# Scaling attention probabilities on another engine, and turning two heads of a short branch at once

## The chip, the cores and the metric

The kernel runs on one core of a Trainium2 chip. The core has TensorE (PE in the profile: matrix products and transposes, with weight loads listed apart as PEld), VectorE (DVE), ScalarE (ACT), GpSimd (POOL) and SyncE (SP, which here issues every DMA). The metric is the device time of one launch in microseconds (us), lower is better. A measurement of this kernel is told as the median of its runs.

## The reference, cut to what matters

One decoder block on 1024 tokens of width 1024, all in float32: a normalised and modulated input goes through one wide projection; part of its columns feed 16 attention heads in 2 groups of 8, part a state-space mixer (SSD); the two are merged and projected, and a gated feed-forward layer follows. The change concerns the attention. Each query attends in three branches, and each branch is weighted by its own learned gate:

```python
s_c = einsum('btgjd,bngd->bgjtn', qb, k_cmp) * scale          # compressed keys, 63 of them
p_c = masked_softmax(s_c, cmp_end[None, :] <= t[:, None])
o_c = einsum('bgjtn,bngd->btgjd', p_c, v_cmp)
...
p_s = masked_softmax(s_s, m_s)                                # selected blocks
o_s = einsum('bgjtk,bgtkd->btgjd', p_s, vg)
...
p_w = masked_softmax(s_w, m_w)                                # sliding window of 512
o_w = einsum('bgjtk,bkgd->btgjd', p_w, vwb)
o = gb[..., 0:1] * o_c + gb[..., 1:2] * o_s + gb[..., 2:3] * o_w
```

With 1024 tokens, 16 blocks of 64 keys and 16 blocks chosen, the selected branch sees every earlier key.

## The kernel before, in words

The program has a projection stage (to about 260 us), an attention stage (about 260 to 1340 us), the SSD stage (to about 1860 us) and the feed-forward tail. Attention works in 32 units: group `g`, tile `i` of 128 queries, and half `hq` of the group's heads, so 4 heads of 128 queries each. A unit has three branches: `br` 0 (selected, `i + 1` tiles of 128 keys), `br` 1 (window, at most 5 tiles) and `br` 2 (compressed, 64 columns of which 63 count).

For branches 0 and 1, `score` makes for each head the product of queries and keys (`S`, two matmuls, since values are kept as a high and a low part), adds the mask and finds the row's extreme on VectorE (L1707, tile `P`), and takes the exponential in place on ScalarE with its row sums (L1711). After the fourth head, one reciprocal of the sums (L1717) and four instructions `scale` (L1720), one a head, multiply the 128 x n probabilities in place by the inverse sum and by the gate, two numbers a row. `score_cmp` does the same for the 4 heads of branch 2 in one tile `Pc` of 128 x 4 x 64.

`value_step` then turns the probabilities: PE transposes one 128 x 128 block of each of 4 heads into a tile `tp` (L1787); ScalarE copies `tp` rounded into the first half of a pair (L1790), VectorE subtracts that to get the second half (L1791, both named `kv` since the pairs lie in the buffer of keys and values). For branch 2 the block is 64 columns wide, so `tp` has 64 rows in use, again 4 transposes. `products` multiplies each half by the values and sums all tiles of the unit in one PSUM tile `o` (L1018): two matmuls of 512 columns a step, with 64 rows of `cvc` (compressed values) for branch 2 and 128 rows of `kv` otherwise.

The order on all engines is fixed when the program is built, by a planner (`Flow`). It walks through a model of time: each operation has a cost in us written beside it, times a reserve of 1.15 on ScalarE and VectorE and 1.2 on GpSimd, and a latency behind it. PE takes what is ready of the streams `products`, `scores` and `values`, in that rank, and a background stream `F` fills the rest: the projections of the SSD inputs (`fps`) and what follows them, such as the convolution, three instructions of L1064 and one of L1080 on VectorE for each 128 x 512 block of 24 of them. Every engine then runs its own list strictly in order. In the attention stage GpSimd computes the low parts of weights (L311, `wlo`) and, in 8 stretches (`mod_rows`), row sums of `w_ada`: four products (L1276, `wada`) and eight sums (L1279, `acc`), whose input comes by DMA. The probabilities of branch 0 have 4 buffers (tags a1 and a2), those of branch 1 another 4 (tag b): a buffer is free again when the last transpose of its branch has run.

Of the kernel before, what the change touches and what calls it, by code (L numbers as in the profile page):

```python
# [37 lines left out]
K_MLE, K_TGT, K_COS, K_SIN, K_RV, K_ID, K_END = 0, 128, 256, 320, 384, 392, 520  # L38
# [186 lines left out]
class Kern:  # L225
# [93 lines left out]
    def rope(self, x, nh, t):  # L319
# [3 lines left out]
        cb = self.kc[:, K_COS + 8 * t:K_COS + 8 * t + 8][:, None, :].to_broadcast(sh)  # L323
        sb = self.kc[:, K_SIN + 8 * t:K_SIN + 8 * t + 8][:, None, :].to_broadcast(sh)
# [34 lines left out]
    def startup(self):  # L359
# [70 lines left out]
        self.kcop = D(1.5, [], self.load_constants)  # L430
# [110 lines left out]
    def projections(self):  # L541

        nc, a, wk, dr, cp = self.nc, self.a, self.wk, self.dr, self.cp
        self.kc = wk.tile([128, K_ID], F, name="kc")
# [4 lines left out]
        self.tgt = self.kc[:, K_TGT:K_TGT + 128]  # L549
# [28 lines left out]
                          ("kv", 0), ("kv", 1))] + [Stream(self.token_blocks())])  # L578

# [39 lines left out]
    def q_evac(self, b, t0, ps, op):  # L619
# [15 lines left out]
        r = V(1.65, [x, self.kcop], rot)  # L635
        d = D(0.7, [r], store)
# [3 lines left out]
    def kv_evac(self, kind, t0, ps, op):  # L640
# [34 lines left out]
        r = V(1.75, [k1, self.kcop], rot)  # L675
        self.turns.append((kind, t0, [(kk, r)] + ([(vs, v1)] if kind == 0 else [])))
# [87 lines left out]
    def gates_dt(self):  # L764
# [67 lines left out]
        for lt, dst in ((self.mle, self.eac), (self.tgt, self.etl), (self.ones, self.edc)):  # L832
            ps = self.buf("t", [128, 256], "cum")
            op = yield ([dop, ps], 0.43, lambda lt=lt, ps=ps: nc.tensor.matmul(ps.t, lt, daf(), start=True, stop=True))
# [35 lines left out]
    def compress(self):  # L870
# [3 lines left out]
        self.cvc = wk.tile([64, 2, 2, 64], FR, name="cvc")  # L874
# [5 lines left out]
    def compress_part(self, m):  # L880
# [62 lines left out]
        else:  # L943
            for g in range(2):
                vp = self.buf("t", [64, 64], "vcp")

                def mm(g=g, vp=vp):
                    for t in range(2):
                        nc.tensor.matmul(vp.t, hs[:, t, g], w2[:, t], start=t == 0, stop=t == 1)

                op = yield (ev + [c["d2"], vp], 0.22, mm)
                y = A(0.11, [op], lambda g=g, vp=vp: nc.scalar.activation(self.cvc[:, g, 0], vp.t, AF.Copy))
                self.cvcop = V(0.14, [y], lambda g=g, vp=vp: nc.vector.tensor_sub(self.cvc[:, g, 1], vp.t, self.cvc[:, g, 0]))
                vp.until(self.cvcop)
            w2.until(op)
# [51 lines left out]
    def products(self, units):  # L1007
# [3 lines left out]
        for u in units:  # L1011
            o = self.buf("o", [128, 4, 128], f"o{u.nm}")
            for n in range(u.total):
                while not self.pv:
                    yield None
                vst, rows, pair, hi, lo = self.pv.pop(0)
                for m, need in ((0, hi), (1, lo)):
                    op = yield ([need, o], 0.22, lambda n=n, m=m, vst=vst, rows=rows, pair=pair: nc.tensor.matmul(  # L1018
                        o.t, vst(), pair()[m][:rows], start=n + m == 0, stop=n == u.total - 1 and m == 1))
# [31 lines left out]
    def background(self):  # L1051
# [7 lines left out]
        def finish_x(ps, op, ft, h):  # L1059
# [566 lines left out]
class Unit:  # L1626
# [51 lines left out]
    def score(self, br, h):  # L1678
# [315 lines left out]
```

## Time and profile before

| | |
|---|---|
| median of 3 runs | 2702.74 us (2699.96 to 2707.79) |
| the profiled execution, its own time | 2705.52 us |
| its span from first to last instruction | 2703.7 us |
| mean granted TensorE clock | 0.977 of full speed |
| busy: PE / DVE / ACT / POOL | 95% / 64% / 43% / 25% of the span |

The page gives busy time and idle time by engine over the whole span; the stage that the change touches is 40% of it, so views of the stretch from 260 to 1340 us are used where a number is to be about that stage. A granted clock of 1.0 means 2.4 GHz, 0.5 means 1.2 GHz. The time of a matmul runs to its modelled end, so the distance between the starts of neighbouring matmuls tells what one costs in a row.

### The profile page before, as it was taken

What the parts mean: (1) busy time and instruction counts of PE and PEld (TensorE: products, weight loads), DVE (VectorE), ACT (ScalarE), POOL (GpSimd) and SP (SyncE); (2) the same over time, 40 slices, a digit from 0 to 9 for tenths busy, and PEclk for the clock granted to TensorE, in tenths of its full rate; (3) what the DMA queues carried; (4) which work ended last, traced back from release to release, by engine and by line L of the source; (5) the groups of instructions that cost most, each with busy time, mean ns of one, the idle gap of its engine ahead of it and who ended that gap; (6) DMA issues with size and microseconds to landing.
All of it is one profiled execution on the core that took longest, in us unless ns stands there. A gap on an engine that the chain in (4) does not pass through costs nothing.

```text
span 2703.7 us, 38173 instructions
## 1 busy us (share of the span) xinstructions
PE 2581.8 (95%) x14098; PEld 2185.0 (81%) x14098; DVE 1737.9 (64%) x4053; ACT 1152.5 (43%) x2458; POOL 664.0 (25%) x397
## 2 busy tenths in 40 slices
PE   6999999989998999999998999989999999999997
PEld 5999778878887888887877888769988888888885
DVE  7644987887886888877557579877722333333336
ACT  4322665556564655665545355542621111111113
POOL 2112222131222232312242322212122112222223
PEclk8999999999999999999998999989999999999999
DMA  6434232222223232212455544335221111111111
GB/s 234 142 105 143 85 86 63 64 78 71 63 67 126 86 92 73 90 43 71 138 164 190 188 139 129 106 122 171 73 77 40 39 47 47 47 47 47 47 55 63
DMA packets 206555, 253.95 MB, mean 94 GB/s; under 512 B 15256, under 2 KB 150040, under 8 KB 205856
## 3 DMA queue, kind: packets, MB, share of 16 engines
q1 hardware_dynamic: 206368, 251.51, 29.9%
q8 instruction: 111, 1.82, 0.3%
q14 instruction: 76, 0.62, 0.1%
HBM read 195.75 MB, written 55.71 MB: 93 GB/s over the span
## 4 chain that ended last, share of the span: by engine, by line
PE 79%; DVE 13%; DMA 3%; ACT 3%; issue 2%; SPq 0%; POOL 0%; DVEq 0%; ACTq 0%; POOLq 0%
PE fps L280 6%; PE gu L280 6%; PE fps L282 6%; PE fps L281 6%; PE gu L281 6%; PE gu L282 6%; PE o L1018 5%; PE tp L1787 4%; PE S L1702 4%; DVE P L1720 3%; PE dps L282 3%; PE dps L281 3%; PE dps L280 3%; PE yd L1905 2%; PE tokps L282 2%
## 5 line engine op out<-in xcount | busy, mean ns | idle before, releaser
L1569 DVE TENSOR_TENSOR x<-x,dps 128x512 f32<-128x512 f32 x176 | 120.9, 687 | 248.8 <-PE dps L282 248.6
L280 PE MATMUL gu<-m_hi,whi_w 128*128 128x512 f32 x704 | 279.8, 397 | 0.0
L281 PE MATMUL gu<-m_lo,whi_w 128*128 128x512 f32 x704 | 276.2, 392 | 0.0
L282 PE MATMUL gu<-m_hi,wlo_w 128*128 128x512 f32 x704 | 274.6, 390 | 0.0
L1790 ACT ACTIVATE kv<-tp 128x512 fp32r<-128x512 f32 (+1 forms) x296 | 172.9, 595 | 228.0 <-PE tp L1787 204.9
L311 POOL TENSOR_TENSOR wlo_w<-raw_w,whi_w 128x1024 fp32r<-128x1024 f32 x44 | 109.5, 2509 | 533.3 <-ACT whi_w L309 533.3
L1791 DVE TENSOR_TENSOR kv<-tp,kv 128x512 fp32r<-128x512 f32 (+1 forms) x296 | 196.7, 684 | 51.2 <-ACT kv L1790 50.0
L1018 PE MATMUL o<-kv 128*128 128x512 f32 x528 | 193.4, 420 | 12.5 <-DVE kv L1791 9.7
L1711 ACT ACTIVATE P<-P,sm 128x640 f32<-128x640 f32 (+7 forms) x256 | 186.5, 730 | 33.7 <-DVE sm L1707 32.4
L1702 PE MATMUL S<-kv,Q 128*128 128x384 f32 (+5 forms) x768 | 185.8, 344 | 6.7 <-DVE sm L1707 6.5
L1720 DVE TENSOR_SCALAR P<-P,sm,gate 128x640 f32<-128x640 f32 (+7 forms) x256 | 188.5, 800 | 1.2
L1787 PE MATMUL tp<-id,P 128*128 128x128 f32 x1056 | 157.9, 277 | 9.5 <-DVE Q L1666 5.9
L280 PE MATMUL fps<-hT_hi,whi_x 128*128 128x512 f32 x384 | 159.7, 416 | 4.0 <-ACT xs L1105 3.3
L282 PEld LDWEIGHTS gu<-m_hi,wlo_w 128*128 128x128 f32 x704 | 132.3, 188 | 33.0
L1787 PEld LDWEIGHTS tp<-id,P 128*128 128x128 f32 x1056 | 128.3, 142 | 37.5 <-issue 11.2
L280 PEld LDWEIGHTS gu<-m_hi,whi_w 128*128 128x128 f32 x704 | 132.1, 188 | 29.9
L281 PEld LDWEIGHTS gu<-m_lo,whi_w 128*128 128x128 f32 x704 | 131.8, 187 | 30.3
L282 PE MATMUL fps<-hT_hi,wlo_x 128*128 128x512 f32 x384 | 152.6, 397 | 0.0
L281 PE MATMUL fps<-hT_lo,whi_x 128*128 128x512 f32 x384 | 152.5, 397 | 0.0
L280 PE MATMUL fps<-whi_z,hT_hi 128*128 128x256 f32 x512 | 150.8, 295 | 0.9 <-ACT u L1067 0.6
L1702 PEld LDWEIGHTS S<-kv,Q 128*128 128x128 f32 x768 | 129.8, 194 | 24.0 <-DVE sm L1707 9.9
L1707 DVE CUSTOM_DVE_ANT_0 P<-S,kb 128x256 f32<-128x256 f32 (+5 forms) x256 | 120.5, 493 | 42.7 <-PE tp L1787 32.8
(342 smaller groups left out, 7046.7 us busy)
## 6 DMA issues: line engine op xcount, KB each, us to landing
wada<-w_ada SPq DMA_DIRECT2D x40, 512.0 KB, 4.3
ac<-acd SPq DMA_DIRECT2D x32, 512.0 KB, 4.9
raw_x<-w_in SPq DMA_DIRECT2D x24, 512.0 KB, 5.1
raw_w<-w_gate SPq DMA_DIRECT2D x22, 512.0 KB, 4.3
raw_w<-w_up SPq DMA_DIRECT2D x22, 512.0 KB, 3.8
rawd<-w_down SPq DMA_DIRECT2D x22, 512.0 KB, 3.8
xsd<-xs SPq DMA_DIRECT2D x32, 256.0 KB, 2.4
raw_z<-w_in SPq DMA_DIRECT2D x16, 512.0 KB, 4.7
```

Source lines behind the costliest of these rows:

```text
L280: mm(ps, lh, rh, start=k == 0, stop=False)
L281: mm(ps, lh, rl, start=False, stop=False)
L282: mm(ps, ll, rh, start=False, stop=k == kt - 1)
L1018: op = yield ([need, o], 0.22, lambda n=n, m=m, vst=vst, rows=rows, pair=pair: nc.tensor.matmul(o.t, vst(), pair()[m][:rows], start=n + m ...
L1569: e = V(0.6, [op], lambda ps=ps, t=t, cs=cs: nc.vector.tensor_tensor(self.x1[:, t, cs], self.x1[:, t, cs], ps.t, op=OP.add))
L1702: mm(sp[:, :w], q, kvb.kv[:, br, r, first + c0:first + c1], start=r == 0, stop=r == 1)
L1707: nc.vector.tensor_tensor_reduce(P[:, c0:c1], sp[:, :w], k.kb[:, m0:m0 + w], scale=-1.0, scalar=sm[:, 0, h:h + 1] if p else 3.0e38, op0=OP ...
L1711: ex = A(0.26 + 0.8333e-3 * n, [mx], lambda: nc.scalar.activation(P[:, :n], P[:, :n], AF.Exp, bias=sm[:, 1, h:h + 1], scale=-1.0, accum_ou ...
L1720: nc.vector.tensor_scalar(P[:, :n], P[:, :n], sm[:, 3, m:m + 1], k.gate[:, i, self.h0 + m, br + 1:br + 2], op0=OP.mult, op1=OP.mult)
L1787: nc.tensor.transpose(tp[:rows, h], P, k.id)
L1790: hi = A(0.48, [op, pair], lambda: nc.scalar.activation(pair()[0][:rows], tp[:rows], AF.Copy))
L1791: lo = V(0.6, [hi], lambda: nc.vector.tensor_sub(pair()[1][:rows], tp[:rows], pair()[0][:rows]))
```

## The change

Four edits. First, `scale` runs on GpSimd and is booked there at 0.25 + 1.08e-3 n us. Second, branch 2 turns two heads with one transpose: two neighbouring heads of `Pc` are one block of 128 columns, so a step has 2 transposes and a `tp` of 128 x 256, and the copies of the pair shrink to 256 columns. The values of that branch lie in `cvc` once in the upper 64 rows and once in the lower 64, with zeros in the other half, and each half of the pair is multiplied by both, 256 columns each, into every second head of `o`. Third, `compress_part` makes these doubled values (a doubled `hs2`, a memset on GpSimd). Fourth, to make room for them, the rotary tables and one mask move from the constants into a buffer of tag a1, which is free between the start and the attention; and the planner's costs for the convolution and for the products are raised.

```diff
             def scale(m=m, P=self.P[br, m][0]):
-                nc.vector.tensor_scalar(P[:, :n], P[:, :n], sm[:, 3, m:m + 1], k.gate[:, i, self.h0 + m, br + 1:br + 2],
+                nc.gpsimd.tensor_scalar(P[:, :n], P[:, :n], sm[:, 3, m:m + 1], k.gate[:, i, self.h0 + m, br + 1:br + 2],
                                         op0=OP.mult, op1=OP.mult)
-            self.P[br, m] = self.P[br, m][0], V(0.2 + 0.55e-3 * n, [e], scale)
+            self.P[br, m] = self.P[br, m][0], G(0.25 + 1.08e-3 * n, [e], scale)
...
+        n = 2 if br == 2 else 4
+        c = slice(0, 128 * n)
...
         def trans():
-            for h in range(4):
-                P = self.P[2, 0][0][:, h] if br == 2 else self.P[br, h][0][:, j * 128:(j + 1) * 128]
-                nc.tensor.transpose(tp[:rows, h], P, k.id)
+            for h in range(n):
+                P = self.P[2, 0][0][:, 2 * h:2 * h + 2].rearrange("p h n -> p (h n)") if br == 2 \
+                    else self.P[br, h][0][:, j * 128:(j + 1) * 128]
+                nc.tensor.transpose(tp[:, h * 128:h * 128 + 128], P, k.id)
...
+                def product(m, n=n, vst=vst, pair=pair, o=o, u=u):
+                    if vst is None:
+                        for r in range(2):
+                            nc.tensor.matmul(o[:, r::2], self.cvc[:, u.g, r].rearrange("n r d -> n (r d)"),
+                                             pair()[m][:, 0:256], start=False, stop=False)
...
-                    op = yield ([need, o], 0.22, lambda n=n, m=m, vst=vst, rows=rows, pair=pair: nc.tensor.matmul(
+                    op = yield ([need, o], 0.23 if vst else 0.24, lambda m=m, product=product: product(m))
...
-            c = V(2.25, [a0, a1, e], conv)
+            c = V(2.5, [a0, a1, e], conv)
...
-            f = V(0.66, [th], lambda: nc.vector.scalar_tensor_tensor(u.t, xr[:, 3:], 1.0, u.t, op0=OP.add, op1=OP.mult))
+            f = V(0.75, [th], lambda: nc.vector.scalar_tensor_tensor(u.t, xr[:, 3:], 1.0, u.t, op0=OP.add, op1=OP.mult))
...
-        nc.sync.dma_start(self.kc, a["kc"][:, 0:K_ID])
+        nc.sync.dma_start(self.kc, a["kc"][:, 0:K_COS])
+        nc.sync.dma_start(self.kt.t, a["kc"][:, K_COS:K_ID])
```

On VectorE near the end of the attention of the second group (unit `7_0`, branch 1; `Pc` and `st` belong to its branch 2, `S_7_1` to the next unit) the list before reads:

```order
L1717 RECIPROCAL sm_7_0_13026<-sm_7_0_13026 128x4
L1791 TENSOR_TENSOR kv_8653<-tp_7_0_13189,kv_8653 128x512
L1720 TENSOR_SCALAR P_7_0_13111<-P_7_0_13111,sm_7_0_13026,gate 128x640
L1720 TENSOR_SCALAR P_7_0_13116<-P_7_0_13116,sm_7_0_13026,gate 128x640
L1720 TENSOR_SCALAR P_7_0_13145<-P_7_0_13145,sm_7_0_13026,gate 128x640
L1720 TENSOR_SCALAR P_7_0_13172<-P_7_0_13172,sm_7_0_13026,gate 128x640
L1747 RECIPROCAL st_7_0_13162<-st_7_0_13162 128x4
L1748 TENSOR_TENSOR st_7_0_13162<-st_7_0_13162,gate 128x4
L1749 TENSOR_TENSOR Pc_7_0_13194<-Pc_7_0_13194,st_7_0_13162 128x256
L1791 TENSOR_TENSOR kv_8653<-tp_7_0_13234,kv_8653 128x512
```

In the changed program the same stretch of VectorE's list (L1754 is the reciprocal of the sums, L1784 to L1786 the scaling of `Pc`, L1828 the subtraction) reads:

```order
L1754 RECIPROCAL sm_7_0_12952<-sm_7_0_12952 128x4
L1784 RECIPROCAL st_7_0_13104<-st_7_0_13104 128x4
L1785 TENSOR_TENSOR st_7_0_13104<-st_7_0_13104,gate 128x4
L1786 TENSOR_TENSOR Pc_7_0_13121<-Pc_7_0_13121,st_7_0_13104 128x256
L1828 TENSOR_TENSOR kv_8506<-tp_7_0_13152,kv_8506 128x512
```

The four scalings stood ahead of the scaling of the compressed branch and of the next subtractions, and are gone from this list. On GpSimd, in the last of the 8 stretches of `mod_rows`, the list before has only the products and sums of `w_ada`:

```order
L1276 TENSOR_TENSOR wada_13309<-wada_13309,sc 128x1024
L1279 TENSOR_TENSOR acc_13221<-acc_13221,wada_13309 128x512
L1276 TENSOR_TENSOR wada_13345<-wada_13345,sc 128x1024
L1279 TENSOR_TENSOR acc_13221<-acc_13221,wada_13309 128x512
L1279 TENSOR_TENSOR acc_13221<-acc_13221,wada_13345 128x512 x2
```

At the same place of GpSimd's list in the changed program (unit `7_1`, branch 0; L1757 is `scale`, L1313 and L1316 are the products and sums) there stands:

```order
L1757 TENSOR_SCALAR P_7_1_13268<-P_7_1_13268,sm_7_1_13117,gate 128x1024
L1313 TENSOR_TENSOR wada_13331<-wada_13331,sc 128x1024
L1313 TENSOR_TENSOR wada_13366<-wada_13366,sc 128x1024
L1316 TENSOR_TENSOR acc_13278<-acc_13278,wada_13331 128x512
L1757 TENSOR_SCALAR P_7_1_13275<-P_7_1_13275,sm_7_1_13117,gate 128x1024
L1316 TENSOR_TENSOR acc_13278<-acc_13278,wada_13331 128x512
L1757 TENSOR_SCALAR P_7_1_13308<-P_7_1_13308,sm_7_1_13117,gate 128x1024
L1316 TENSOR_TENSOR acc_13278<-acc_13278,wada_13366 128x512
L1757 TENSOR_SCALAR P_7_1_13333<-P_7_1_13333,sm_7_1_13117,gate 128x1024
```

The scalings of one branch now lie between products that wait for a DMA.

## Rows read from the trace of the kernel before

**Rows 1.** The page: its first line, and busy time by engine over the span.
```profile
span 2703.7 us, 38173 instructions
PE 2581.8 (95%) x14098; PEld 2185.0 (81%) x14098; DVE 1737.9 (64%) x4053; ACT 1152.5 (43%) x2458; POOL 664.0 (25%) x397
```
**Rows 2.** Busy time of each engine by stretch of the attention stage: stretch and its length, then busy us (and instructions) of PE, PEld, DVE, ACT, POOL, the granted TensorE clock, DMA share, GB/s. The last row is a stretch of the fifth, asked for by itself.
```profile
260.00:400.00 140.00, 130.69 (x662) 105.01 (x661) 124.94 (x285) 90.41 (x234) 40.95 (x29) 0.96 0.31 88
400.00:600.00 200.00, 190.17 (x1165) 165.84 (x1163) 167.62 (x355) 113.50 (x260) 50.56 (x33) 0.96 0.23 67
600.00:800.00 200.00, 192.96 (x1208) 169.04 (x1209) 170.99 (x373) 120.39 (x247) 52.54 (x34) 0.98 0.24 70
800.00:1000.00 200.00, 189.02 (x1182) 164.18 (x1181) 154.73 (x369) 112.28 (x300) 45.46 (x29) 0.97 0.31 97
1000.00:1200.00 200.00, 194.81 (x1123) 166.44 (x1122) 168.77 (x390) 119.30 (x259) 56.07 (x36) 1.00 0.25 76
1200.00:1340.00 140.00, 136.95 (x707) 111.74 (x705) 98.12 (x218) 78.98 (x168) 36.67 (x21) 0.99 0.28 86
sum 1080.00, PE 1034.61 PEld 882.25 DVE 885.17 ACT 634.86 POOL 282.24; mean PE 172.44 PEld 147.04 DVE 147.53 ACT 105.81 POOL 47.04
...
1100.00:1200.00 100.00, 100.00 (x531) 83.52 (x530) 80.41 (x197) 62.00 (x134) 28.54 (x18) 1.00 0.25 77
```
**Rows 3.** What PE waited for between 260 and 1340 us: who, for whom, us in total, times, longest. The view has 13 rows. Nine name DVE, 39.5 us together, of which the longest and the shortest stand below; four name ACT, 5.4 us together, of which the longest stands below.
```profile
PE o L1018 <- DVE kv L1791: 10.0, 6, 5.6
...
PE fps L280 <- ACT xs L1105: 3.6, 2, 3.3
...
PE fps L280 <- DVE zu L1121: 0.7, 1, 0.7
```
**Rows 4.** The scaling on DVE: the page's group of all 256 (busy us, mean ns, idle before), the shortest, median and longest of all forms, and two of its forms by themselves.
```profile
L1720 DVE TENSOR_SCALAR P<-P,sm,gate 128x640 f32<-128x640 f32 (+7 forms) x256 | 188.5, 800 | 1.2
...
L1720 DVE TENSOR_SCALAR P<-P,sm,gate x256: 327/607/3009, 270.5 to 1307.8; 128x640 f32<-128x640 f32 x40, 128x128 f32<-128x128 f32 x16, 128x256 f32<-128x256 f32 x16, 128x384 f32<-128x384 f32 x16
...
L1720 DVE TENSOR_SCALAR P<-P,sm,gate 128x640 f32<-128x640 f32 x80 | 66.1, 888 | 0.3
L1720 DVE TENSOR_SCALAR P<-P,sm,gate 128x896 f32<-128x896 f32 x16 | 10.9, 743 | 0.1
```
**Rows 5.** One stall in the order of time (start us, duration us, engine, line, instruction; in brackets idle time before it and who ended it).
```profile
1266.64 6.31 DVE L1720 TENSOR_SCALAR P<-P,sm,gate 128x640 f32<-128x640 f32 x4
...
1266.99 4.10 POOL L1276 TENSOR_TENSOR wada<-wada,sc 128x1024 f32<-128x1024 f32 x2 [37.48 <-DMA wada<-w_ada]
...
1273.07 1.02 DVE L1748 TENSOR_TENSOR st<-st,gate 128x4 f32<-128x4 f32 x1
...
1275.20 1.10 PE L1018 MATMUL o<-kv 128*128 128x512 f32 x3 [2.38 <-DVE kv L1791]
...
1277.90 0.63 PE L281 MATMUL fps<-hT_lo,whi_m 128*128 128x512 f32 x1
```
**Rows 6.** The convolution and the subtraction on DVE over the whole program: count, then ns of the shortest, the median and the longest.
```profile
L1064 DVE SCALAR_TENSOR_TENSOR u<-xr,hcw,u x144: 716/752/2872, 257.0 to 1124.8; 128x512 f32<-128x512 f32 x144
...
L1080 DVE SCALAR_TENSOR_TENSOR u<-xr,u x48: 678/691/2924, 260.1 to 1127.1; 128x512 f32<-128x512 f32 x48
...
L1791 DVE TENSOR_TENSOR kv<-tp,kv x296: 659/684/693, 278.8 to 1332.2; 128x512 fp32r<-128x512 f32 x128, 64x512 fp32r<-64x512 f32 x20
```
**Rows 7.** Instructions of GpSimd by group (busy us, mean ns, idle before and who ended it), and the two groups of the convolution.
```profile
L1279 POOL TENSOR_TENSOR acc<-acc,wada 128x512 f32<-128x512 f32 x64 | 89.9, 1405 | 3.6
L1276 POOL TENSOR_TENSOR wada<-wada,sc 128x1024 f32<-128x1024 f32 x32 | 63.0, 1978 | 271.1 <-DMA wada<-w_ada 271.1
...
L1270 POOL MEMSET acc<- 128x512 f32 x8 | 4.2, 524 | 0.0
...
L1064 DVE SCALAR_TENSOR_TENSOR u<-xr,hcw,u 128x512 f32<-128x512 f32 x144 | 129.4, 898 | 11.7 <-ACT u L1067 7.9
...
L1080 DVE SCALAR_TENSOR_TENSOR u<-xr,u 128x512 f32<-128x512 f32 x48 | 41.1, 857 | 12.3 <-ACT xr L1079 11.9
```
**Rows 8.** PE instructions in order of time, for the distance between starts: a matmul of 512 columns, a group of 4 transposes and what follows it, and matmuls of 256 columns.
```profile
1184.98 0.39 PE L282 MATMUL fps<-hT_hi,wlo_m 128*128 128x512 f32 x1
1185.21 0.60 PE L1787 MATMUL tp<-id,P 128*128 128x128 f32 x4
1185.57 0.48 PE L280 MATMUL fps<-hT_hi,whi_m 128*128 128x512 f32 x1
1185.88 0.40 PE L281 MATMUL fps<-hT_lo,whi_m 128*128 128x512 f32 x1
...
420.07 0.28 PE L281 MATMUL fps<-wlo_z,hT_hi 128*128 128x256 f32 x1
420.19 0.28 PE L282 MATMUL fps<-whi_z,hT_lo 128*128 128x256 f32 x1
```
**Rows 9.** The compressed branch between 260 and 1340 us: its transposes and products on PE, its subtraction on DVE, and a subtraction of 256 columns for comparison.
```profile
L1018 PE MATMUL o<-kv,cvc 64*128 64x512 f32 x64 | 30.2, 489 | 0.3 <-DVE kv L1791 0.3
...
L1787 PE MATMUL tp<-id,Pc 128*64 128x128 f32 x128 | 21.0, 291 | 4.5 <-DVE Pc L1749 4.5
...
L1791 DVE TENSOR_TENSOR kv<-tp,kv 64x512 fp32r<-64x512 f32 x32 | 21.7, 678 | 2.8 <-ACT kv L1790 2.5
...
L1666 DVE TENSOR_TENSOR Q<-tq,Q 64x256 fp32r<-64x256 f32 x32 | 13.7, 427 | 0.5
```

More of the change, by code (lines that the diff above doesn't have):

```diff
@@ L543, in projections @@
         nc, a, wk, dr, cp = self.nc, self.a, self.wk, self.dr, self.cp
-        self.kc = wk.tile([128, K_ID], F, name="kc")
+        self.kc = wk.tile([128, K_COS], F, name="kc")
         self.kb = wk.tile([128, B_END], BF, name="kb")
@@ L548, in projections @@
         self.mle = self.kc[:, K_MLE:K_MLE + 128]
-        self.tgt = self.kc[:, K_TGT:K_TGT + 128]
+        self.kt = self.buf("a1", [128, K_ID - K_COS], "kt")
+        self.ktuse = []
         self.kvd = [dr.tile([128, 2, 3, 1024], FR, name=f"kvd{g}") for g in range(2)]
@@ L635, in q_evac @@
         r = V(1.65, [x, self.kcop], rot)
+        self.ktuse.append(r)
         d = D(0.7, [r], store)
@@ L831, in gates_dt @@
         daf = lambda: sp[1][:, 2].rearrange("p c h -> p (c h)")
-        for lt, dst in ((self.mle, self.eac), (self.tgt, self.etl), (self.ones, self.edc)):
+        tgt = lambda: self.kt[:, K_TGT - K_COS:K_TGT - K_COS + 128]
+        for lt, dst in ((lambda: self.mle, self.eac), (tgt, self.etl), (lambda: self.ones, self.edc)):
             ps = self.buf("t", [128, 256], "cum")
-            op = yield ([dop, ps], 0.43, lambda lt=lt, ps=ps: nc.tensor.matmul(ps.t, lt, daf(), start=True, stop=True))
+            op = yield ([dop, ps], 0.43, lambda lt=lt, ps=ps: nc.tensor.matmul(ps.t, lt(), daf(), start=True, stop=True))
+            self.ktuse.append(op)
             def decay(dst=dst, ps=ps):
@@ L873, in compress @@
         self.ckc = wk.tile([128, 2, 2, 64], FR, name="ckc")
-        self.cvc = wk.tile([64, 2, 2, 64], FR, name="cvc")
+        self.cvc = wk.tile([128, 2, 2, 2, 64], FR, name="cvc")
+        self.cvz = self.fl.op(2, 0.5, [], lambda: self.nc.gpsimd.memset(self.cvc.bitcast(F), 0.0))
         for m in range(2):
@@ L943, in compress_part, with twice, high, low @@
         else:
+            h2 = self.buf("c7", [128, 2, 2, 2, 64], "hs2")
+            def twice():
+                for r in range(2):
+                    nc.vector.tensor_copy(h2[:, :, :, r], hs.t)
+            x = V(0.35, ev + [h2], twice)
             for g in range(2):
-                vp = self.buf("t", [64, 64], "vcp")
+                vp = self.buf("t", [128, 64], "vcp")
                 def mm(g=g, vp=vp):
                     for t in range(2):
[L949 to L953, printed above, removed]
+                        nc.tensor.matmul(vp.t, h2[:, t, g].rearrange("p r n -> p (r n)"), w2[:, t], start=t == 0, stop=t == 1)
+                def high(g=g, vp=vp):
+                    for r in range(2):
+                        b = slice(64 * r, 64 * r + 64)
+                        nc.scalar.activation(self.cvc[b, g, r, 0], vp[b], AF.Copy)
+                def low(g=g, vp=vp):
+                    for r in range(2):
+                        b = slice(64 * r, 64 * r + 64)
+                        nc.vector.tensor_sub(self.cvc[b, g, r, 1], vp[b], self.cvc[b, g, r, 0])
+                op = yield ([x, c["d2"], vp], 0.22, mm)
+                y = A(0.46, [op, self.cvz], high)
+                self.cvcop = V(0.46, [y], low)
                 vp.until(self.cvcop)
+            h2.until(op)
             w2.until(op)
@@ L1015, in products @@
                     yield None
-                vst, rows, pair, hi, lo = self.pv.pop(0)
+                vst, pair, hi, lo = self.pv.pop(0)
+                def product(m, n=n, vst=vst, pair=pair, o=o, u=u):
+                    if vst is None:
+                        for r in range(2):
+                            nc.tensor.matmul(o[:, r::2], self.cvc[:, u.g, r].rearrange("n r d -> n (r d)"),
+                                             pair()[m][:, 0:256], start=False, stop=False)
+                    else:
+                        nc.tensor.matmul(o.t.rearrange("p h q -> p (h q)"), vst(), pair()[m], start=n + m == 0, stop=n == u.total - 1 and m == 1)
                 for m, need in ((0, hi), (1, lo)):
-                    op = yield ([need, o], 0.22, lambda n=n, m=m, vst=vst, rows=rows, pair=pair: nc.tensor.matmul(
-                        o.t, vst(), pair()[m][:rows], start=n + m == 0, stop=n == u.total - 1 and m == 1))
+                    op = yield ([need, o], 0.23 if vst else 0.24, lambda m=m, product=product: product(m))
                 pair.until(op)
```

27 lines of the change are left out of this document (13 added, 14 removed).

## The prediction

> **What bounds the kernel now.** I read the page's busy times first [rows 1]: PE is busy for 95% of the span, so there is little idle time, and the change can win what PE does, what PE waits, and what the granted clock takes from it. Since only the attention stage changes, the next view is the busy time by stretch [rows 2]. From 260 to 1340 us PE is busy 1034.6 of 1080 us, so it is idle for 45.4 us. The clock column gives the second loss: at 0.96 for 140 us, 0.96, 0.98, 0.97 and 1.00 for 200 us each and 0.99 for 140 us, (1 - clock) times length adds up to 5.6 + 8 + 4 + 6 + 0 + 1.4 = 25 us of work not done at full clock. Loss in this stage is thus about 70 us. DVE is busy 885.2 us here, 82%, GpSimd 282.2 us, 26%.
>
> The view of waits says who ends the idle time [rows 3]: nine of 13 rows name DVE, 39.5 us together, four name ACT, 5.4 us. So PE is the bound and DVE, in order and 82% busy, is the engine that comes late. The group of the scaling tells why [rows 4]. An instruction of 128 x 896 takes 743 ns in the mean, the shortest one, 128 x 128, 327 ns: between the two lies 0.54 ns a column and a fixed 0.26 us. The 256 instructions have 4 heads x 4 halves of groups x 66 tiles x 128 = 135,168 columns, so undisturbed they would take 256 x 0.26 + 135,168 x 0.54 ns = 67 + 73 = 140 us. They take 188.5 us, and the longest 3009 ns. The stall in order of time shows how [rows 5]: four scalings of 640 columns, 4 x 0.61 = 2.4 us undisturbed, take 6.31 us while GpSimd runs two products of `w_ada`, the next DVE instruction of 4 elements a row takes 1.02 us, PE then stands for 2.38 us for the subtraction queued behind them, and after it a matmul takes 0.63 us instead of the 0.39 to 0.40 us in [rows 8], so the clock has dropped to its lower level.
>
> **The change, part by part.**
>
> The scaling leaves DVE: -188.5 us of its time. On DVE the compressed step shrinks too: 32 subtractions of 678 ns become ones of 256 columns, nearest row 427 ns, -8 us [rows 9]. Against this stands what GpSimd's new work blocks. The convolution shows it: median 752 ns but mean 898, and 691 but 857 [rows 6, 7], so 144 x 146 + 48 x 166 ns = 29 us are lost now, while GpSimd is 26% busy. The subtraction L1791 runs at 659 to 693 ns throughout, so it isn't touched. With GpSimd at 46% (next part) the 29 us grow to about 29 x 46 / 26 = 51, +22 us. DVE comes to 885 - 188 - 8 + 22 = 711 us, 66% of the stage.
>
> The Trainium skill, "SBUF — State Buffer", section "Who interferes with whom", says that a DVE instruction with two SBUF inputs contends with a GpSimd instruction that reads SBUF, and that whoever comes second waits to the end. The rows of the convolution agree (up to 2872 ns), and by that rule no edit here removes the contention, it only moves the scaling to its other side; the 22 us are that part of the sum.
>
> The scaling arrives on GpSimd: 256 instructions. No row shows this operation there, so I bound it. Below stands the memset of 512 columns, 524 ns, which reads nothing, 1.02 ns a column; above, the sum of two tensors of 512 columns, 1405 ns, 2.74 ns a column [rows 7]. The product with one number a row, 1978 ns for 1024 columns, lies between, at 1.93. The scaling reads one tensor and writes it in place, and so is nearest to the memset; I take what the planner books, 0.25 + 1.08e-3 n us (0.80 us for 512), which gives 256 x 0.25 + 135,168 x 1.08 ns = 210 us. With 282 that is 492 us, 46% of the stage: no queue that is full. The bounds of the sum are 135,168 x 1.02 = 138 and x 2.74 = 370 us.
>
> What that does to PE is the main term. Four scalings of 640 columns take 4 x 0.94 = 3.8 us on GpSimd against a measured 4 x 0.888 = 3.6 us on DVE: the probabilities are ready at about the same time, but the subtractions, the maxima and the scaling of the compressed branch no longer queue behind them. How much of DVE's 39.5 us goes I bound by nothing and all of it. The row for 1100 to 1200 us, where the convolution is over but for its first part, has DVE at 80%, no idle time on PE and a clock of 1.00 [rows 2]; at 66% I therefore take two thirds, -26 us, and keep a third for bursts of the convolution. The clock's 25 us follow from stalls as in [rows 5], so again two thirds: -16 us. What is late next is GpSimd's own list: where scalings lie between products of `w_ada`, the wait for the DMA (271 us in all now, in front of an engine that had nothing else to do [rows 7]) and each 1.98 us product stand before probabilities that PE needs. That happens in 8 stretches; about one product's half each, +1 us of PE time a stretch, between 0 (the planner put background work there) and 4 us (two products): +8 us.
>
> The compressed branch: 128 transposes become 64. Four of them take 0.36 us from start to start, and the matmul after them starts 0.31 us before its successor instead of 0.23, so 0.36 + 0.08 = 0.44, 0.11 us each [rows 8]: -64 x 0.11 = -7.0 us. The 64 products of 512 columns (0.23 us from start to start) become 128 of 256 (0.12 us): 64 x 0.01 = +0.6 us [rows 8, 9]. Together -6.4 us, all on PE. ACT copies half as much in 32 steps; ACT waits anyway for PE, so nothing.
>
> The doubled values, the memset and the moved tables cost some four small instructions on DVE and ACT and one more DMA in the first 260 us, ahead of everything that waits for them: nothing, or 1 us if the first rotation came to wait. The planner's raised costs change where background work is put, not how much there is: nothing.
>
> Sum: -26 - 16 + 8 - 6.4 = -40 us from the execution's own 2705.5 us (span 2703.7 and 1.8 around it), 2665; that execution lies 2.8 us above the median, so **2662 us** is forecast for the median. The ends: nothing of the stalls goes and each of the 8 stretches costs 4 us, 2702.7 - 6.4 + 32 = 2728; all 45.4 and 25 us go, 2702.7 - 6.4 - 70.4 = 2626.
>
> **Rivals.**
>
> *The stall only moves* (about 2698). PE waits 45 us in 1080; each wait is ended by the last of a chain, and if the chain then ends on GpSimd at the same time, the idle time keeps its size and only its name changes. For it: the scaling takes as long as before, 3.8 against 3.6 us a branch, and GpSimd's list now holds DMA waits. Against it: the longest group of waits is for the subtraction, not for the scaling. The price is 2702.7 - 6.4 + 2 = 2698. The Trainium skill, "Perfetto Trace Analysis", section "Optimizing Scalar/DVE Operations", warns that GpSimd and DVE share an SBUF read port, so that moving work between them might not help; [rows 5] shows that the shared port is real here, and also that DVE loses by it now, so I give that rule this rival and no more.
>
> *GpSimd's scaling runs at its two-tensor rate* (about 2736, slower). Place: GpSimd, between the reciprocal and the transposes, 64 times. At 2.74 ns a column a scaling of the mean 528 columns takes 1.45 us, four 5.8 us. The planner books 1.2 x (0.25 + 0.57) = 0.98 us, 3.9 for four, and so puts the transposes 1.9 us too early: 64 x 1.9 = 122 us. As PE itself runs behind where it waits, I take half, +60; DVE's relief is halved, -21; transposes -6.4: 2702.7 + 33 = 2736. It decides from 1.2 x 0.82 / 528 = 1.86 ns a column on. The product at 1.93 ns speaks for it, the memset at 1.02 against. The Trainium skill, "GPSIMD Engine Reference", section "Engine selection", has both sides: about twice as slow as VectorE with two inputs, roughly line rate with one. By the second half of that sentence this rival falls; no row here shows a one-input operation.
>
> *All of it comes back* (about 2630): DVE at 66% is never late, ACT's 5 us remain. The 100 us stretch without any idle time speaks for it, the bursts of the convolution and [rows 3] with ACT against.
>
> **How the numbers follow.** The forecast's case, 2640 to 2692, gets 0.58; all comes back, below 2640, 0.10; the stall only moves, 2692 to 2711, 0.17; GpSimd is too slow, above 2711, 0.15. A measurement of this kernel can tell a difference of about 0.3%, 8 us, from none: 2694.6 to 2710.8. Faster takes the first two cases and a third of the third, 0.73; within 0.3% 0.12; slower 0.15. The range that holds 8 in 10 leaves out half of the case below and most of the slow one: 2634 to 2712; the likeliest case alone has 2640 to 2692.
>
> **What would show it.** In the profile after, the scaling on GpSimd should have a mean near 0.82 us for its mean of 528 columns; above 0.98 us the second rival is on. DVE should be busy about 710 us in the attention stage and its convolution have a mean a little above 898 ns. PE's idle time there should fall from 45 to about 27 us (45 - 26 + 8), the wait of the products for the subtraction first of all, and the clock should show 0.98 to 1.00 in most stretches. The prediction is wrong if PE's waits name GpSimd or the transposes for more than 20 us, or if idle time and clock stay and only the 6 us of transposes are won. The stages before 260 and after the attention should keep their length to 3 us.

## The result and the profile after

The changed kernel takes 2636.35 us in the median of 4 runs (2632.65 to 2637.57), the kernel before beside it 2702.89 us: a ratio of 0.975, 95% interval 0.9732 to 0.9767, 66.5 us less where 40 were forecast. The profiled execution has 2636.85 us, a span of 2635.0 us and a mean clock of 0.985.

The head of its page, as [rows 1]:

```profile
PE 2535.0 (96%) x14098; PEld 2169.0 (82%) x14098; DVE 1584.9 (60%) x3801; ACT 1149.3 (44%) x2460; POOL 876.1 (33%) x654
```

The attention stage in stretches, with the columns of [rows 2]; the last stretch is shorter, since the stage now ends before 1280 us:

```profile
260.00:400.00 140.00, 132.34 (x706) 109.38 (x706) 118.23 (x276) 98.19 (x263) 74.36 (x76) 1.00 0.33 95
400.00:600.00 200.00, 196.54 (x1280) 175.61 (x1279) 158.29 (x376) 132.33 (x293) 88.30 (x80) 1.00 0.22 66
600.00:800.00 200.00, 194.21 (x1301) 175.28 (x1301) 136.79 (x307) 113.14 (x251) 98.64 (x80) 1.00 0.33 98
800.00:1000.00 200.00, 198.51 (x1268) 177.52 (x1267) 152.18 (x383) 132.80 (x340) 106.56 (x107) 1.00 0.28 87
1000.00:1200.00 200.00, 197.42 (x1132) 170.66 (x1131) 131.60 (x316) 116.40 (x240) 87.04 (x69) 1.00 0.23 72
1200.00:1290.00 90.00, 90.00 (x467) 74.71 (x465) 43.00 (x103) 49.49 (x104) 45.33 (x31) 1.00 0.47 142
sum 1030.00, PE 1009.02 PEld 883.16 DVE 740.09 ACT 642.35 POOL 500.23; mean PE 168.17 PEld 147.19 DVE 123.35 ACT 107.06 POOL 83.37
```

The clock is 1.00 in every stretch, where before only one long stretch had that. PE is idle for 1030 - 1009 = 21 us instead of 45. DVE went from 885 us (to 1340) to 740 us (to 1290), GpSimd from 282 to 500; up to 1274 us, where the next stage starts, it is 729 and 492.

What PE waited for between 260 and 1290 us, the view of [rows 3]; the longest five:

```profile
PE o L1053 <- DVE kv L1828: 11.3, 11, 2.2
PE S L1739 <- DVE sm L1744: 3.3, 4, 1.3
PE o L1050 <- DVE kv L1828: 2.7, 3, 1.1
PE o L1053 <- DVE ot L1067: 1.2, 2, 0.9
PE tp L1824 <- DVE Pc L1786: 0.7, 1, 0.7
```

No row of the view names GpSimd. The scaling on its new engine by size, as in [rows 4] (busy us, mean ns; behind it the idle time and who ended it):

```profile
L1757 POOL TENSOR_SCALAR P<-P,sm,gate 128x640 f32<-128x640 f32 x80 | 75.0, 949 | 106.8 <-DVE sm L1754 85.1 <-PE tp L1824 13.0 <-DVE st L1784 8.6
L1757 POOL TENSOR_SCALAR P<-P,sm,gate 128x512 f32<-128x512 f32 x32 | 26.4, 842 | 49.0 <-DVE sm L1754 39.6 <-DVE st L1784 9.4
...
L1757 POOL TENSOR_SCALAR P<-P,sm,gate 128x1024 f32<-128x1024 f32 x16 | 19.2, 1214 | 62.2 <-DVE sm L1754 62.2
...
L1757 POOL TENSOR_SCALAR P<-P,sm,gate 128x128 f32<-128x128 f32 x32 | 16.5, 532 | 31.3 <-DVE sm L1754 25.7 <-DVE st L1784 4.5 <-ACT kv L1827 1.1
```

All 256 take 215.8 us, mean 857 ns. Most of GpSimd's idle time before them ends when DVE's reciprocal (L1754) comes, so there GpSimd is not late.

Where the stage ends shows in the first matmul of the SSD stage (`yd`), in the view of that tile, first before, then after (count, ns of the shortest, median and longest, first and last start):

```profile
L1905 PE MATMUL yd<-xs,E x512: 217/275/421, 1339.8 to 1813.5; 128*128 128x64 f32 x171
```
```profile
L1942 PE MATMUL yd<-xs,E x512: 217/275/421, 1274.1 to 1744.6; 128*128 128x64 f32 x171
```

From 1339.8 to 1274.1: 65.7 of the span's 68.7 us were won by the end of the attention stage, the other 3 behind it. The stage itself is 68.3 us shorter, since its first `S` starts 2.6 us later.

### The profile page after: what moved, and what is told of

Read it like the earlier page. It is cut to its first block, busy times and chain, and to the rows that moved or that the text cites. A ratio compares the mean times of both kernels' runs of the same rounds, so it can differ in the third digit from the quotient of the medians.

```text
span 2635.0 us, 38689 instructions
## 1 busy us (share of the span) xinstructions
PE 2535.0 (96%) x14098; PEld 2169.0 (82%) x14098; DVE 1584.9 (60%) x3801; ACT 1149.3 (44%) x2460; POOL 876.1 (33%) x654
## 4 chain that ended last, share of the span: by engine, by line
PE 55%; DVE 4%; DMA 1%; ACT 1%; issue 1%; POOL 0%; SPq 0%; DVEq 0%; ACTq 0%; POOLq 0%
PE gu L280 6%; PE gu L281 6%; PE gu L282 6%; PE dps L282 3%; PE dps L281 3%; PE dps L280 3%; PE fps L280 3%; PE fps L282 3%; PE fps L281 3%; PE yd L1942 2%; PE sps L280 2%; PE sps L281 2%; PE sps L282 2%; PE o L1053 1%; PE tp L1824 1%; PE aps L280 1%
## 5 line engine op out<-in xcount | busy, mean ns | idle before, releaser
L1757 POOL TENSOR_SCALAR P<-P,sm,gate 128x640 f32<-128x640 f32 (+7 forms) x256 | 215.8, 857 | 369.1 <-DVE sm L1754 295.5
L1828 DVE TENSOR_TENSOR kv<-tp,kv 128x512 fp32r<-128x512 f32 (+1 forms) x296 | 189.5, 657 | 115.4 <-ACT kv L1827 114.0
L1827 ACT ACTIVATE kv<-tp 128x512 fp32r<-128x512 f32 (+1 forms) x296 | 165.1, 574 | 190.2 <-PE tp L1824 183.7
L1748 ACT ACTIVATE P<-P,sm 128x640 f32<-128x640 f32 (+7 forms) x256 | 186.8, 732 | 47.5 <-DVE sm L1744 44.9
L1101 DVE SCALAR_TENSOR_TENSOR u<-xr,hcw,u 128x512 f32<-128x512 f32 x144 | 140.4, 976 | 16.3 <-ACT u L1104 11.4
```

The costliest lines, as they stand in the source:

```text
L1101: nc.vector.scalar_tensor_tensor(u.t, xr[:, k:k + N2], hcw[:, ft, k:k + 1], u.t, op0=OP.mult, op1=OP.add)
L1748: ex = A(0.26 + 0.8333e-3 * n, [mx], lambda: nc.scalar.activation(P[:, :n], P[:, :n], AF.Exp, bias=sm[:, 1, h:h + 1], scale=-1.0, accum_ou ...
L1757: nc.gpsimd.tensor_scalar(P[:, :n], P[:, :n], sm[:, 3, m:m + 1], k.gate[:, i, self.h0 + m, br + 1:br + 2], op0=OP.mult, op1=OP.mult)
L1827: hi = A(0.064 + 0.104 * n, [op, pair], lambda: nc.scalar.activation(pair()[0][:, c], tp[:, c], AF.Copy))
L1828: lo = V(0.068 + 0.133 * n, [hi], lambda: nc.vector.tensor_sub(pair()[1][:, c], tp[:, c], pair()[0][:, c]))
```

## The experiments

Eleven runs in three groups; the kernel before measured 2700.97, 2702.31 and 2699.46 us beside them, and each ratio is to the one of its group. One table holds the reading of the profiled executions of ten of them (with two passes on GpSimd, PE idles for 285 us, much of it at the lower clock, and the reading below doesn't hold). The stage is from the weight load of the first `S` to the first `yd`. "At 1.2 GHz" is the time in it at the lower clock level, half of which is lost. "Background" is how many `fps` matmuls of 512 columns more than in before the order places in the stage (0.23 us each, [rows 8]). PE's own work is the stage less idle time, less half of the time at 1.2 GHz, less that background: what is left is what the instructions of the attention cost on PE. It is good to some 5 us: the four kernels in which those instructions are the same as before have 1002 to 1009, the six with the whole compressed branch 973 to 983.

| kernel | median us | stage | idle | at 1.2 GHz | background | PE's own work |
|---|---|---|---|---|---|---|
| before | 2702.7 | 1073.7 | 44.9 | 51.2 | 0 | 1003 |
| only bookings raised | 2689.3 | 1076.0 | 43.1 | 36.8 | +36 | 1006 |
| raised bookings, scaling booked nearer | 2693.2 | 1125.6 | 35.6 | 20.5 | +309 | 1009 |
| only scaling on GpSimd | 2671.5 | 1040.4 | 25.1 | 27.3 | 0 | 1002 |
| only products of 128 rows | 2679.5 | 1046.1 | 43.5 | 20.5 | +27 | 986 |
| scaling and products | 2664.1 | 1035.6 | 30.4 | 23.9 | +27 | 987 |
| only the compressed branch | 2693.6 | 1052.3 | 61.1 | 47.8 | -24 | 973 |
| all but the bookings | 2651.5 | 1004.4 | 26.5 | 6.8 | -18 | 979 |
| scaling on ScalarE | 2653.5 | 1053.1 | 31.1 | 13.7 | +141 | 983 |
| one multiplication on GpSimd | 2674.3 | 1044.8 | 48.7 | 30.7 | -6 | 982 |
| scaling booked as measured | 2656.2 | 1025.2 | 37.6 | 23.9 | -6 | 977 |
| **after** | 2636.4 | 1005.4 | 21.0 | 0.0 | +15 | 981 |

**The scaling alone**, in the kernel before.

```diff
-                nc.vector.tensor_scalar(P[:, :n], P[:, :n], sm[:, 3, m:m + 1], ...
+                nc.gpsimd.tensor_scalar(P[:, :n], P[:, :n], sm[:, 3, m:m + 1], ...
-            self.P[br, m] = self.P[br, m][0], V(0.2 + 0.55e-3 * n, [e], scale)
+            self.P[br, m] = self.P[br, m][0], G(0.25 + 1.08e-3 * n, [e], scale)
```

> The kernel before with one edit: the scaling runs on GpSimd and is booked there at 0.25 + 1.08e-3 n us. Theory A (DVE's relief is the gain): about 2645 us, some 58 us of the 66; no stretch of the attention stage below a clock of 0.99, PE idle there under 28 us. Theory B (the planner's raised bookings give slack, the scaling only part of it): about 2675 us. Theory C (the compressed branch gives most): 2690 us or more.

2671.46 us, ratio 0.9882 (0.9864 to 0.9899): -29.5. Its waits, longest two:

```profile
PE o L1018 <- DVE kv L1791: 11.8, 7, 2.7
PE S L1702 <- DVE sm L1707: 7.5, 5, 4.4
```

The first theory has its idle time (25 us, under 28) but not its clock and not its time: 2671 is nearest to the number of the second. Idle time falls by 20 us, the lower clock's loss by 12, PE's own work stays. None of its waits names GpSimd.

**The compressed branch alone** (after, with the scaling back on DVE and the old bookings).

```diff
...
-                nc.gpsimd.tensor_scalar(P[:, :n], P[:, :n], sm[:, 3, m:m + 1], ...
+                nc.vector.tensor_scalar(P[:, :n], P[:, :n], sm[:, 3, m:m + 1], ...
-            self.P[br, m] = self.P[br, m][0], G(0.25 + 1.08e-3 * n, [e], scale)
+            self.P[br, m] = self.P[br, m][0], V(0.2 + 0.55e-3 * n, [e], scale)
```

> The changed kernel with the scaling back on DVE at its old booking, and the old bookings for convolution and products: only the two heads that share a transpose are left. Theory A: 2703 - 6 = about 2697 us, with the clock dropping in the attention stage as before. Theory C: 2680 us or less, since DVE and ACT are spared 256 columns in 32 steps.

2693.63 us, 0.9969 (0.9955 to 0.9983): -7.3, which looks like the forecast's -6.4. The table says otherwise: PE's own work falls by 30 us and idle time rises by 16. The waits show DVE still late, and later than before:

```profile
PE o L1053 <- DVE kv L1828: 22.8, 11, 4.9
PE xsT L1132 <- DVE mod L1339: 9.2, 2, 8.4
```

**The raised bookings alone.**

```diff
-                    op = yield ([need, o], 0.22, ...
+                    op = yield ([need, o], 0.23, ...
-            c = V(2.25, [a0, a1, e], conv)
+            c = V(2.5, [a0, a1, e], conv)
-            f = V(0.66, [th], ...
+            f = V(0.75, [th], ...
```

> The kernel before with the planner's bookings raised as in the change (convolution 2.5 and 0.75 us, products 0.23 us) and nothing else. Theory A: no difference, 2703 us within 8. Theory B: 2685 us or less, because the order then fits what DVE really takes.

2689.27 us, 0.9947 (0.9929 to 0.9965): -11.7, though no instruction changed. It falls between the two theories. The stage isn't shorter; it holds 36 more background matmuls, and less time at 1.2 GHz.

**After with the old bookings.**

```diff
-                    op = yield ([need, o], 0.23 if vst else 0.24, ...
+                    op = yield ([need, o], 0.22 if vst else 0.24, ...
-            c = V(2.5, [a0, a1, e], conv)
+            c = V(2.25, [a0, a1, e], conv)
-            f = V(0.75, [th], ...
+            f = V(0.66, [th], ...
```

> The changed kernel with the old bookings for convolution and products. Theory A: as the changed kernel, 2637 us within 8. Theory B: 2655 us or more.

2651.45 us, 0.9808 (0.9786 to 0.9831). This too falls between the two theories; in this order the bookings are worth 15 of the 66 us.

**The raised bookings, and the scaling booked on DVE nearer to what it measures.**

```diff
-            self.P[br, m] = self.P[br, m][0], V(0.2 + 0.55e-3 * n, [e], scale)
+            self.P[br, m] = self.P[br, m][0], V(0.45 + 0.55e-3 * n, [e], scale)
```

> The kernel before with raised bookings as in the run on the bookings alone (2689 us), and in addition the scaling, still on DVE, booked at 0.45 + 0.55e-3 n us, near the 0.80 us that it takes in the mean. Theory A (DVE's load and its bursts cost the time): 2689 us within 8, since DVE has the same work. Theory B (the order was made for a DVE that is faster than the real one): 2675 us or less, and the clock no longer drops in the attention stage.

2693.22 us, 0.9964 (0.9951 to 0.9977), no better than the raised bookings alone, as the first theory had it. The order changes a good deal (309 more background matmuls in a stage 52 us longer than before), the time doesn't. So the gain is not had by planning with a truer number alone.

**Two passes on GpSimd**, each with one number a row.

```diff
-                nc.gpsimd.tensor_scalar(P[:, :n], P[:, :n], sm[:, 3, m:m + 1], k.gate[:, i, self.h0 + m, br + 1:br + 2], op0=OP.mult, op1=OP.mult)
+                nc.gpsimd.tensor_scalar(P[:, :n], P[:, :n], sm[:, 3, m:m + 1], None, op0=OP.mult)
+                nc.gpsimd.tensor_scalar(P[:, :n], P[:, :n], k.gate[:, i, self.h0 + m, br + 1:br + 2], None, op0=OP.mult)
```

> The changed kernel, but GpSimd scales in two passes, one for the inverse sum and one for the gate, each 0.26 to 1.2 us, at the booking of one: GpSimd's work for the scaling doubles to some 430 us and four scalings of 640 columns take 7.6 us. If the rival on a slow GpSimd had its price right (half of what the booking falls short, here 64 x 3 us): 2636 + 95 = about 2730 us. If PE's background work covers such delays: 2650 us or less.

3006.68 us, 1.112 (1.1096 to 1.1145). The groups of the two passes, and PE's longest waits:

```profile
L1757 POOL TENSOR_SCALAR P<-P,sm 128x640 f32<-128x640 f32 x80 | 153.5, 1919 | 65.3 <-DVE sm L1754 38.5 <-DVE st L1784 16.7 <-PE tp L1824 10.2
L1758 POOL TENSOR_SCALAR P<-P,gate 128x640 f32<-128x640 f32 x80 | 151.9, 1899 | 7.5
...
PE tp L1824 <- POOL P L1758: 203.1, 74, 6.8
PE tp L1824 <- POOL xr L1108: 23.4, 9, 5.3
```

Both expected numbers, 2730 and 2650, missed. One pass takes twice what the pass with two numbers takes. GpSimd is busy for 1099 of 1380 us, 80%, and PE waits for it: the place of the second rival.

**The scaling on ScalarE** (DVE makes inverse sum times gate first, one small instruction for 4 heads; new bookings left out below).

```diff
...
+            nc.vector.tensor_tensor(sm[:, 3], sm[:, 3], k.gate[:, i, self.h0:self.h0 + 4, br + 1], op=OP.mult)
...
-                nc.gpsimd.tensor_scalar(...
+                nc.scalar.activation(P[:, :n], P[:, :n], AF.Copy, scale=sm[:, 3, m:m + 1])
```

> The changed kernel, but ScalarE scales, by one number a row that DVE makes from inverse sum and gate, booked as the exponential is. Theory A: DVE's relief counts and not the engine that takes the work, so 2640 to 2665 us, with ScalarE at some 90% of the attention stage; the convolution on DVE back at a mean below 898 ns, since GpSimd reads less. If ScalarE becomes the late engine: 2690 us or more.

2653.48 us, 0.9825 (0.9803 to 0.9847), in the range of the theory that DVE's relief counts, on whichever engine the work lands. Two misses: ScalarE was expected at some 90% and is busy for 780 of 1050 us, 74%, and the convolution's mean was expected below 898 ns and is 1012.

**Products of 128 rows alone** (the compressed branch as in after, scaling and bookings as before, but four transposes and copies of 512 columns again, two of them repeats that no product reads).

```diff
-        n = 2 if br == 2 else 4
+        n = 4
...
-                P = self.P[2, 0][0][:, 2 * h:2 * h + 2]...
+                P = self.P[2, 0][0][:, 2 * (h % 2):2 * (h % 2) + 2]...
```

> The kernel with the two heads that share a transpose (2694 us), but with four transposes and copies of 512 columns a step as before, two of the four being repeats that nothing reads: only the products with 128 rows are left of the change. If the products with 64 rows hold PE up (distances of 0.32, 0.42 and 0.34 us around one instead of 0.23 each, so 64 x 0.39 = up to 25 us): PE has at least 17 us less work in the attention stage than before. If transposes and copies are what the change saves: no difference to the kernel before.

2679.48 us, 0.9915 (0.9896 to 0.9935): -23 us from products that the forecast had priced at +0.6. PE's own work falls from 1003 to 986. But the four transposes of this run are of 128 columns, where those of before have 64 (`128*64`), so the run changes two things at once. The order of time in before tells them apart, first what a 64-row product does to its neighbours (start, duration):

```profile
1100.44 0.40 PE L282 MATMUL fps<-hT_hi,wlo_x 128*128 128x512 f32 x1
1100.76 0.49 PE L1018 MATMUL o<-kv,cvc 64*128 64x512 f32 x1
1101.18 0.50 PE L280 MATMUL fps<-hT_hi,whi_x 128*128 128x512 f32 x1
1101.52 0.39 PE L281 MATMUL fps<-hT_lo,whi_x 128*128 128x512 f32 x1
1101.75 0.40 PE L282 MATMUL fps<-hT_hi,wlo_x 128*128 128x512 f32 x1
```

and four products of 128 rows and 256 columns in after:

```profile
1002.83 0.40 PE L1053 MATMUL o<-kv 128*128 128x512 f32 x1
1003.06 0.62 PE L1050 MATMUL o<-kv,cvc 128*128 128x256 f32 x4
1003.52 0.51 PE L1739 MATMUL S<-kv,Q 128*128 128x384 f32 x2
```

Before, the starts are 0.32, 0.42 and 0.34 us apart around the lone product, 0.23 behind that: 3 x 0.23 = 0.69 became 1.08, 0.39 us more for one change to 64 rows and back. After, the matmul ahead keeps its 0.23, and four products take 0.46, 0.115 each.

Two products of 64 rows in a row, in before, and four transposes of 64 columns:

```profile
1208.08 0.40 PE L1018 MATMUL o<-kv 128*128 128x512 f32 x1
1208.40 0.73 PE L1018 MATMUL o<-kv,cvc 64*128 64x512 f32 x2
1209.07 0.66 PE L1787 MATMUL tp<-id,P 128*128 128x128 f32 x4
1209.48 0.47 PE L1702 MATMUL S<-kv,Q 128*128 128x448 f32 x1
...
278.60 0.39 PE L282 MATMUL fps<-hT_hi,wlo_x 128*128 128x512 f32 x1
278.83 0.60 PE L1787 MATMUL tp<-id,Pc 128*64 128x128 f32 x4
279.18 0.48 PE L280 MATMUL fps<-hT_hi,whi_x 128*128 128x512 f32 x1
279.50 0.39 PE L281 MATMUL fps<-hT_lo,whi_x 128*128 128x512 f32 x1
```

The pair pays once: 0.32 + 0.67 + 0.41 = 1.40 us where 0.23 + 0.46 + 0.36 = 1.05 are usual. The transposes pay nothing: 0.23 us ahead of them, 0.35 for four and 0.32 for the matmul behind, as for those of 128 columns in [rows 8] (0.36 and 0.31). So the 17 us belong to the products.

**Scaling and products, without the halved transposes** (after with the old bookings, and this).

```diff
-        n = 2 if br == 2 else 4
+        n = 4
```

> The kernel after with the planner's old costs and with four transposes and copies of 512 columns a step again (two of the four are repeats that no product reads), so what is left of the change is the scaling on GpSimd and the products of 128 rows. Theory (the 64-row products hold PE up by some 20 us in all, and this adds to the relief of DVE; the transposes are the 7 us that the prediction counted): 2671 - 23 = 2648 from the scaling alone, or the run with old costs plus 7, 2658; 2645 to 2660. Rival (the transposes to 64 partitions are what held PE up, not the products): most of those 20 us stay, about 2668. Rival (the two reliefs only add up because the shorter copies take load from DVE): between, 2655 to 2668, with DVE named in more than 25 us of PE's waits.

2664.08 us, 0.986 (0.984 to 0.9881), above the 2645 to 2660 expected, near the rivals' numbers. By the time alone the transposes would have won 12.6 us and the products 7. By PE's own work it is 987, as in the run with the products alone (986): the products' share stands, and only idle time and clock (30.4 and 23.9 us, against 26.5 and 6.8) ate the rest. The rival that the transposes to 64 partitions hold PE up isn't tested here, since these transposes have 128 columns; it falls by the distances shown above. The last rival, that the two reliefs only add up because the shorter copies relieve DVE, has its numbers met: the time, and over 25 us of waits that name DVE, 26.1 between 260 and 1340 us. But with the shorter copies they are 25.2, so that row doesn't tell the two apart, and this share stays open.

**One multiplication on GpSimd, by one number a row** (the product of the two made on DVE as for ScalarE).

```diff
-                nc.gpsimd.tensor_scalar(P[:, :n], P[:, :n], sm[:, 3, m:m + 1], k.gate[:, i, self.h0 + m, br + 1:br + 2], op0=OP.mult, op1=OP.mult)
+                nc.gpsimd.tensor_scalar(P[:, :n], P[:, :n], sm[:, 3, m:m + 1], None, op0=OP.mult)
```

> The kernel after with one multiplication of the probabilities on GpSimd by one number a row: DVE multiplies the inverse sum by the gate first (4 elements a row, 64 more instructions). By the run with two passes, one such pass of 640 columns takes 1.9 us where the pass with two numbers takes 0.95. Theory: the form with one number is the slow one, also when it comes alone; the scaling has a mean near 1.6 us, 400 us in all, GpSimd is some 700 us busy in the attention stage, and four scalings take 6.4 us where 3.9 are booked. By the prediction's law (half of what the booking falls short) 2636 + 64 x 2.5 / 2 = 2716; by the 0.65 of it that the two passes cost, 2740. Rival (the two passes were slow because the second one waited on the first one's rows, not by their form): mean near 0.85 us and 2633 to 2645. Rival (what decides is whether GpSimd's queue fills up, and at two thirds busy it doesn't): mean near 1.6 us but 2645 to 2690, with GpSimd named in less than 25 us of PE's waits.

2674.34 us, 0.9897 (0.9877 to 0.9917): +38 against after, still 25 us faster than before.

```profile
L1761 POOL TENSOR_SCALAR P<-P,sm 128x640 f32<-128x640 f32 (+7 forms) x256 | 416.8, 1642 | 288.1 <-DVE sm L1756 158.0 <-PE tp L1827 42.6 <-ACT row L1327 17.1
...
PE o L1053 <- DVE kv L1831: 15.5, 10, 2.6
PE tp L1827 <- POOL P L1761: 11.5, 10, 1.9
```

The form with one number is the slow one by itself, 1642 ns in the mean. GpSimd is busy 684 of 1030 us, 66%, and PE waits 12.5 us for it: the numbers of the third theory, that its queue must fill up first, are met.

**The scaling booked as it measures after.**

```diff
-            self.P[br, m] = self.P[br, m][0], G(0.25 + 1.08e-3 * n, [e], scale)
+            self.P[br, m] = self.P[br, m][0], G(0.49 + 0.72e-3 * n, [e], scale)
```

> The kernel after with one number of the planner changed: the scaling is booked as 0.49 us + 0.72 ns a column, which is what the trace after shows in the mean (0.85 us for 512 columns where 0.80 is booked, 0.58 for 128 where 0.39 is). It changes only the order. Theory (bookings move background work and decide some 10 us either way, without a direction that nearness to the truth gives): 2625 to 2650. Rival (booking nearer to the truth is always better): 2615 to 2632.

2656.24 us, 0.9835 (0.9816 to 0.9853): 20 us slower than after, 6 above the range of the first theory and 24 above the rival's. PE's own work is 977 us, its idle time 37.6 and 23.9 us at 1.2 GHz: the same instructions in another order.

## Why the prediction was right, and where its terms were off

The sign and the path were right: DVE's list is relieved, PE's waits for it shrink, the clock gains with them, and GpSimd is not late. The size was not: 66.5 us instead of 40, so that 2636 lies 2 us above the lower end of the range that was to hold 8 in 10 and in the band below 2640, which had a chance of 0.10. In the profiled executions the stage lost 68.3 us: 23.9 of idle time, 51.2 / 2 = 25.6 of clock, 22 of PE's own work, less 3.5 for 15 more background matmuls. The forecast had -26 + 8 = -18, -16 and -6.4.

- **DVE's waits, -26: in the main right.** The rows that name DVE went from 39.5 to 19.9 us, -19.6: half of them, not two thirds. With the scaling alone they come to 23.1. The rest of the 23.9 us is that the waits for ACT, 5.4 us, are nearly gone (0.4), which the forecast had left as they were.
- **GpSimd's list, +8: nothing.** No wait of PE names it. The sizes came out right, 215.8 us for 210, mean 857 ns for 820, GpSimd busy 492 us to the end of the stage, as forecast, but that has luck in it: the booking's law is off at both ends (128 columns take 532 ns where it has 388, 1024 columns 1214 where it has 1356), and the nearness to the memset that it was chosen for fails for the form with one number, which at 3.08 ns a column lies above the upper bound of 2.74. What failed is the step from a queue half full to a wait of PE; even at 66% it was 12.5 us.
- **The clock, -16: mis-sized, -25.6.** "Again two thirds" assumed that what stalls are left still lower it. That stalls lower it is borne out: in before, each of the stage's ten stretches at 1.2 GHz starts in a wait of PE of 2.0 to 5.6 us or at most 1.3 us behind one. In the stage after, the longest single wait is 2.2 us, and the clock never fell; but length alone doesn't decide, since with the scaling alone it fell beside waits of 1.6 and 1.7 us. The scaling alone gives half, 51.2 to 27.3 us at 1.2 GHz, the scaling with the compressed branch 6.8. The gains of the two are 29.5 + 7.3 alone and 49.5 as one. That each lowers the stalls which are left for the other would explain it, but these 13 us are no more than a new order alone moves this kernel by, so it is not shown.
- **The compressed branch, -6.4: the step that failed.** "The 64 products of 512 columns (0.23 us from start to start)" took the distance from matmuls of 128 rows, and passed over the mean of 489 ns in [rows 9], though matmuls of 512 columns in [rows 8] end after 0.39 to 0.40: the row held the 0.1 us that gave the cost away. Measured in PE's own work: -17 for the products (1003 to 986). By the distances in before it is more: of the 64, 50 stand alone and 14 in seven pairs, and nearly all of these 57 places pay 0.34 to 0.40 us, 20 to 22 us in all; the two agree within the 5 us of the table. The transposes come to about -8 (986 to a mean of 979 over the six kernels that have them halved, 973 to 983), where 7 were forecast. The Trainium skill, "TensorEngine Tiling (Array Packing)", section "Key Properties", says that a change of tiling mode, not merely of tile, drains the engine. The distances agree: there is a price on the way in and on the way out. That it is this drain is argued, not shown; no run varied the mode alone, and the transposes of 64 columns show no such price.
- **"The planner's raised costs change where background work is put: nothing" failed too.** -11.7 alone, -15 with the rest, and one other booking +20. A new order of the same instructions moved this kernel by 4 to 20 us, in idle time and clock.
- **DVE, 711 us: 729** to the end of the stage. The convolution lost (976 - 752) x 144 + (977 - 691) x 48 ns = 46 us where the sum had 51; that is a mean near 1010 by the prediction's own law, so its sign of "a little above 898" contradicts its sum. The law, loss in proportion to GpSimd's busy share, isn't borne out: with the scaling on ScalarE GpSimd is no busier than before, and the mean is 1012; with only the bookings raised no instruction changes, and it is 1012 too. The scaling of `Pc` took 608 ns instead of 425, 6 us more; the remaining 17 us were not taken apart.
- **The start, "nothing, or 1 us".** The stage starts 2.6 us later. With only the bookings raised, without any doubled values, it starts 1.9 us later, so most of this is order.
- **The rivals.** "All of it comes back" (2630) is nearest in size, though 21 us of idle time stayed: the products made up for them. "The stall only moves" is refuted by the waits. "GpSimd's scaling runs at its two-tensor rate" had the right place, and a wrong price: past its point of 1.86 ns a column, at 416.8 us / 135,168 = 3.08, the kernel is still faster than before, where 2736 was forecast. PE waits long for GpSimd only in the run where it is 80% busy.

## What to carry to other kernels

When an in-order engine that serves the bound is 82% busy, moving an independent piece to an engine with room can pay twice, in idle time and in the clock; the receiving engine may be slower as long as its list doesn't fill (here it paid at 49% and 66% busy and not at 80%). Look at start-to-start distances around every matmul whose shape differs from its neighbours', not only at those of the common shape. Where a planner sets the order, a difference of less than 20 us between two kernels tells little of one edit: take the engine's work apart from idle time and clock first.

## What was not expected of the hardware

On GpSimd the multiplication of 128 x 640 by two numbers a row takes 949 ns, by one number 1919 ns, and for 1024 columns 1214 against 2846 ns. The form with more arithmetic is the faster one, and the kernel that folded the two numbers into one lost 38 us here. Why the form is slow is open. A matmul of 64 rows between others of 128 delays its own start and the starts of the two behind it, by 0.34 to 0.40 us together, and two in a row delay them no more than one does. A transpose of 64 columns delays nothing.
